# Expert weights in loads of 2 MiB with 16 KB per partition in seven of eleven slots

## The chip, the cores and the metric

The kernel runs on one core of one Trainium2 chip, in one launch. The metric is device time in microseconds of a run. The profile is of one execution; its span is the time from its first to its last instruction.

## The reference

One residual block on x of 256 tokens by 2048 features, all in float32, and a final RMS norm. Shown is the mixture of experts at its end, which the change is about.

```
h = rmsnorm(x); proj = h @ w_in               # 2048 x 11296: gates, SSD inputs, S5 input
... SSD branch -> w_a_up; S5 branch -> w_glu, w_b_up; both gated and summed
x = x + merged @ w_out
h2 = rmsnorm(x, norm_ffn_w)
grp   = argmax(h2 @ w_route_group + b)        # one of 4 groups of 8 experts
top 2 of the 8 experts of that group, softmax weights times the group's probability
for each of 32 experts e, for the tokens that chose it:
    y = (silu(h2 @ w_exp_gate[e]) * (h2 @ w_exp_up[e])) @ w_exp_down[e]
x = x + weighted sum of y;  out = rmsnorm(x, norm_final_w)
```

w_exp_gate and w_exp_up are 2048 x 512 for each expert, w_exp_down is 512 x 2048: 4 MiB each, 12 MiB an expert, 384 MiB for all 32. The other weights come to some 132 MiB.

## The kernel before

Tokens are 256, features 2048 = 16 k-tiles of 128 (KT). The first part streams the dense weights in units of 1 MiB (four k-tiles by 512 columns, rows of 2 KB). SyncE's queue (SP) loads a unit into one of three `raw` buffers; ScalarE and VectorE split it into a high and a low part in two halves, each into one of four `ws` buffers (`hi_next`, `lo_next`); TensorE multiplies (`mm_half`). The main loop (L1344) goes over half units; `hh` is the half, `i` the unit. At the first half of each unit it calls `st.load()` and then `ex_load(1)`. The last 16 units are `w_out`; its left operand lies in four `mg` tiles, and the last four units read one of them each.

The expert stage takes the experts four at a time, in 8 passes `p` (NQ), because at most 32 tokens an expert (CAP) are handled there and 4 x 32 = 128. A pass has: for each quarter `q` of the features, gate then up (L1601: four k-tiles by four experts, 32 matmul instructions as the profile counts them); silu and product; a transposition (L1630); four quarters of down (L1640; in the last pass L1658, in another order). Beside these run the selection of the next pass's tokens, `sel_gen`, in steps that `step(sel)` calls after each gate quarter and after two of the down quarters (four feature tiles a step: sixteen matmuls, L1532, that multiply columns of x1 by a one-hot matrix, then VectorE's scaling by the norm weight, L1536), and `comb` (L1555, L1557), which adds a pass's result to the sum, one quarter at a time after the next pass's gate and up groups. `warm` matmuls (L1437, L1672) are filler.

Which feature stands in which partition of a k-tile is free as long as the weights' rows agree: an expert load puts four successive feature rows of the weight into a partition (`(p k) n -> p k n`, p = 128), and the selection takes the columns of x1 in the same order, at a step of four.

Expert weights lie in `chunks` of 1 MiB: a quarter of one matrix. `EXF` is a queue of free slots; `ex_load(most)` takes slots from its front, each with the next chunk, and issues one DMA on SP; `EXT` remembers which slot holds which chunk; `ex_free` puts a read slot back at the end of the queue. Slots come into being in three ways: 11 tiles of their own, opened at the first unit of w_out in the place of tiles that are no longer needed (`open_out`, L1117); one `mg` tile after each of the last four units (`mg_slot`); `raw` and `ws` buffers when the dense stream lets go of them (`stream_slots`). The three `raw` slots are used once (`keep` false; they hold the sums `accx` and `y` later), the other 19 go round. The order of SP's issues is the order in the program; an issue waits until its slot's readers are done. The last pass's down chunks are cut otherwise, 256 rows by 1024 columns, in rows of 4 KB (L1303).

```
for p in passes:
    for q in 0..3:                     # gate, then up
        for w in (gate, up):
            32 matmuls over 4 k-tiles x 4 experts
            ex_free x 4;  ex_load()
            if w is gate: step(sel)
            one comb of the pass before
    silu, product, transposition
    for k in 0..3: 32 matmuls of down; ex_free x 4; ex_load(); step(sel) at k = 0, 2
```

Of the kernel before, what the change touches and what calls it, by code (L numbers as in the profile page):

```python
# [85 lines left out]
def hybrid_block(tc, A, cst_d, out_d, dbg=None, upto="all"):  # L86
# [949 lines left out]
    def need_v():  # L1036
# [28 lines left out]
    def ev_glu(j):  # L1065
        def f(acc):
# [43 lines left out]
    def open_out():  # L1110
        run_all("ev")
        close(late["gb_m"])
        close(late["ga_m"])
        close(s5_m)
        late["x1p_m"], p = pool("x1p", side="right")
        late["x1p"] = p
        for i in range(EX1):  # L1117
            ex1 = pool(f"ex1{i}", side="right")[1]
            EXF.append(slot_full(ex1, f"ew{i}"))

    def o_add(j, b, acc):
        x = late["x1"][:, b, 512 * j:512 * j + 512]
# [149 lines left out]
    def run_all(*names):  # L1272
        while any([advance(n) is not None for n in names]):
            pass


    chunks = [(w, EQ * p + e, q) for p in range(NQ) for ws in (("w_exp_gate", "w_exp_up"), ("w_exp_down",))
              for q in range(4) for w in ws for e in range(EQ)]
    tail_blocks = len(chunks) - 4 * EQ
    EXF = deque()  # L1280
    EXT = {}
    EXN = {"n": 0}

    def slot_full(pl, tag, keep=True, bufs=1):
        return lambda: pl.tile([P, 4, 512], F32, name="ew", tag=tag, bufs=bufs), keep

    def ex_load(most=99):
        while most > 0 and EXF and EXN["n"] < len(chunks):
            w, e, q = chunks[EXN["n"]]
            slot = EXF.popleft()  # L1290
            t = slot[0]()
            EXT[w, e, q] = (t, slot)
            src = A[w][0, e]
            if w != "w_exp_down":
                SP.dma_start(out=t, in_=src[q * 512:(q + 1) * 512].rearrange("(p k) n -> p k n", p=P))
            elif EXN["n"] < tail_blocks:
                SP.dma_start(out=t, in_=src[q * P:(q + 1) * P].rearrange("p (k n) -> p k n", n=512))
            else:
                h, m = divmod(q, 2)
                src = src[2 * P * m:2 * P * m + 2 * P, 1024 * h:1024 * h + 1024].rearrange("(k p) n -> p k n", p=P)  # L1300
                n = 512 if EXN["n"] == len(chunks) - 1 else 1024
                for c in range(0, 1024, n):
                    SP.dma_start(out=t.rearrange("p (k j) n -> p k (j n)", j=2)[:, :, c:c + n], in_=src[:, :, c:c + n])  # L1303
            EXN["n"] += 1
            most -= 1

    def ex_get(w, e, q):
        return lambda k: EXT[w, e, q][0][:, k]

    def ex_free(w, e, q):  # L1310
        slot = EXT.pop((w, e, q))[1]
        if slot[1]:
            EXF.append(slot)

    def mg_slot(i):
        j = i - (len(st.units) - 4)
        if j >= 0:
            EXF.append(slot_full(late["mgp"], f"mg{j}"))

    freed = {"raw": 0, "ws": 0}  # L1320

    def stream_slots():
        n = len(st.units)
        for tag, bufs, used, done in (("raw", RAWB, len(st.raw), st.nl == n),
                                      ("ws", WSB, len(st.wh) + len(st.split), st.nh == 2 * n)):
            while done and freed[tag] < bufs - used:
                EXF.append(slot_full(wp, tag, keep=tag == "ws", bufs=bufs))
                freed[tag] += 1

    S5_FROM = 9  # L1330
    nu = len(st.units)
# [12 lines left out]
    for hh in range(2 * last_unit):  # L1344
# [16 lines left out]
        if i == nu - 1:  # L1361
            if h == 1:
                last_unit_of_out()
                mg_slot(i)
            stream_slots()
            continue
        acc = mm_half(hh)
        stream_slots()
        if h == 1:
            mg_slot(i)  # L1370
        if i == S5_FROM and h == 0:
            queue("tab", tab_gen())
            queue("rot", rot_gen())
# [133 lines left out]


    nfw = cols[:, VEC["nffn"]:VEC["nffn"] + 16]
    GX = {}  # L1510

    def xg(k, w=1):
# [9 lines left out]
    def sel_gen(p):  # L1522
# [3 lines left out]
        for q in range(4):  # L1526
            n = 2 if p == 0 and q == 0 else 4
            for k0 in range(0, 4, n):
                pt = pe.tile([P, n, P], F32, name="pxg", tag="misc")
                for k in range(n):  # L1530
                    for b in range(2):
                        PE.matmul(pt[:, k], x1[:, b, 512 * q + k0 + k:512 * q + 512:4],  # L1532
                                  gx[:, b].rearrange("p e s -> p (e s)"),
                                  start=(k == 0 and b == 0), stop=(b == 1), skip_group_check=True)
                kk = 4 * q + k0
                V.tensor_tensor(xg(kk, n), pt, nfw[:, kk:kk + n, None].to_broadcast([P, n, P]), op=ALU.mult)  # L1536
# [39 lines left out]
    def step(g):  # L1576
        if g is not None:
            next(g, None)

    def take():  # L1580
        return EXF.popleft()[0]()

    sel = sel_gen(0)
    step(sel)
# [6 lines left out]
    for p in range(NQ):  # L1591
        last = p == NQ - 1
        pg_ = pe.tile([P, 512], F32, name="pg")
        pu_ = pe.tile([P, 512], F32, name="pu")
        for q in range(4):
            for w, o in (("w_exp_gate", pg_), ("w_exp_up", pu_)):
                ch = [ex_get(w, EQ * p + e, q) for e in range(EQ)]
                for k in range(4):
                    kk = 4 * q + k
                    for e, es in enumerate(cols_of):  # L1600
                        PE.matmul(o[es], xg(kk)[:, 0, es], ch[e](k), start=(kk == 0), stop=(kk == KT - 1))  # L1601
                for e in range(EQ):
                    ex_free(w, EQ * p + e, q)
                ex_load()
                if w == "w_exp_gate":
                    step(sel)
                if late_comb:
                    comb(*late_comb.pop(0))
        if last:
            wf = take()  # L1610
            for m in range(4):
# [15 lines left out]
            S.activation(rr[:, 0:1], kcol[:, 0:1], AF.Sqrt)  # L1627
        pt = pe.tile([P, 4, P], F32, name="pat", tag="misc")
        for k in range(4):
            PE.transpose(pt[:, k], sg[:, k * P:k * P + P], ident)  # L1630
# [148 lines left out]
```

## Time and profile before

| | |
|---|---|
| three runs | 1793.95, 1795.37, 1795.83 us; median 1795.37 |
| profiled execution | 1792.91 us, of which its span 1790.8 |
| TensorE busy (matmuls) | 1564.6 us, 87% of the span |
| VectorE, ScalarE, GpSimd busy | 783.7, 569.2, 130.9 us |
| DMA packets | 151,709, 566.05 MB, mean 316 GB/s |
| expert loads | 128 gate, 128 up, 127 down of 1024 KB and 2 of 512 KB; median 19.8 us from issue to landing |

A matmul's busy time is from its start to its modelled end, and these overlap; so 32 matmuls of 0.6 us each can pass in 3.6 us, and a high busy share is not a full engine. "PEld" is TensorE loading its stationary operand. The slices of the page are 44.8 us each. A wait in the profile names the engine that sat idle, the instruction that it then ran, and what released it. "SPq" lines are DMA issues on SyncE's queue: their time is the issue, not the transfer.

### The profile page before, as it was taken

The page shows a single profiled execution, that of the slowest core. Times are in us where ns is not written, and L with a number is a line of the kernel's source. Part 1 is how long each engine was busy: PE and PEld are TensorE (multiplying, and loading weights), DVE is VectorE, ACT ScalarE, POOL GpSimd, SP SyncE. Part 2 cuts the span into 40 slices and gives each one's busy share as a digit, 9 for nine tenths or more (in the row PEclk, how much of TensorE's full clock was granted, in tenths as well). Part 3 has the DMA queues.
Part 4 walks back from the last instruction along what each step waited for, and adds up shares of the span by engine and source line. Part 5 has one row for each costly group of instructions (what it writes and reads, how often), then busy time and mean ns, then how long its engine had stood idle before and what let it go on. Part 6 is the DMA issues. An engine that isn't in the chain of part 4 may idle for free. (4 is left out here: it accounts for less than half of the span.)

```text
span 1790.8 us, 25153 instructions
## 1 busy us (share of the span) xinstructions
PE 1564.6 (87%) x10511; PEld 1072.7 (60%) x10511; DVE 783.7 (44%) x1295; ACT 569.2 (32%) x811; POOL 130.9 (7%) x110
## 2 busy tenths in 40 slices
PE   9999999999999999999978688687687777877876
PEld 8999999999999998988523133132232331322332
DVE  5879888899899895754101101011011010110102
ACT  5465665768865865443000000000000000000003
POOL 3600000101112121000000000000000000000001
PEclk9999999999999998999989989999998998988988
DMA  9666555655566655698899999999999999999995
GB/s 256 215 210 214 187 188 177 196 176 184 182 206 199 190 189 189 213 390 316 340 422 421 421 422 420 421 421 421 421 421 422 421 421 421 422 421 421 421 415 230
DMA packets 151709, 566.05 MB, mean 316 GB/s; under 512 B 22316, under 2 KB 29012, under 8 KB 104232
## 3 DMA queue, kind: packets, MB, share of 16 engines
q1 hardware_dynamic: 149528, 558.74, 81.1%
q0 software_dynamic: 1632, 4.58, 0.9%
q8 instruction: 84, 1.38, 0.3%
q10 hardware_dynamic: 432, 1.08, 0.2%
q14 instruction: 33, 0.27, 0.0%
HBM read 558.04 MB, written 6.32 MB: 315 GB/s over the span
## 5 line engine op out<-in xcount | busy, mean ns | idle before, releaser
L237 PE MATMUL acc<-hTh,ws 128*128 128x256 f32 x1400 | 398.0, 284 | 0.0
L241 PE MATMUL acc<-hTh,ws 128*128 128x256 f32 x1400 | 394.7, 282 | 0.0
L239 PE MATMUL acc<-hTl,ws 128*128 128x256 f32 x1400 | 394.6, 282 | 0.0
L186 DVE TENSOR_TENSOR ws<-raw,ws 128x1024 fp32r<-128x1024 f32 x263 | 328.0, 1251 | 130.3 <-ACT ws L177 129.8
L177 ACT ACTIVATE ws<-raw 128x1024 fp32r<-128x1024 f32 x264 | 277.6, 1056 | 239.4 <-PE acc L241 185.0
L237 PEld LDWEIGHTS acc<-hTh,ws 128*128 128x128 f32 x1400 | 264.0, 189 | 3.9 <-issue 3.5
L239 PEld LDWEIGHTS acc<-hTl,ws 128*128 128x128 f32 x1400 | 263.9, 188 | 0.0
L241 PEld LDWEIGHTS acc<-hTh,ws 128*128 128x128 f32 x1400 | 263.8, 188 | 0.0
L1601 PE MATMUL pg<-ew,xg 128*32 128x512 f32 x1024 | 202.8, 675 | 68.0 <-DMA ew<-in_w_exp_gate_dram 67.8
L1536 DVE TENSOR_TENSOR xg<-pxg,cols 128x512 f32<-128x512 f32 (+1 forms) x33 | 22.3, 675 | 510.6 <-PE pxg L1532 510.6
L1640 PE MATMUL pd<-ew,cstB 128*32 128x512 f32 x896 | 162.8, 670 | 66.8 <-DMA ew<-in_w_exp_down_dram 62.0
L1601 PE MATMUL pu<-ew,xg 128*32 128x512 f32 x1024 | 153.0, 641 | 28.2 <-DMA ew<-in_w_exp_up_dram 28.2
L1601 PEld LDWEIGHTS pg<-ew,xg 128*32 128x32 f32 x1024 | 41.7, 121 | 217.5 <-DMA ew<-in_w_exp_gate_dram 129.0
L1546 ACT ACTIVATE cstC<-pgw 128x256 f32<-128x256 f32 x8 | 3.1, 384 | 522.9 <-PE pgw L1544 522.9
L1640 PEld LDWEIGHTS pd<-ew,cstB 128*32 128x32 f32 x896 | 35.0, 120 | 182.2 <-DMA ew<-in_w_exp_down_dram 116.4
L1532 PEld LDWEIGHTS pxg<-gx,x 128*128 128x128 f32 x512 | 122.0, 328 | 28.4 <-PE pg L1601 17.6
L1532 PE MATMUL pxg<-gx,x 128*128 128x128 f32 x512 | 128.6, 404 | 1.9 <-DVE gx L1519 1.3
L1601 PEld LDWEIGHTS pu<-ew,xg 128*32 128x32 f32 x1024 | 35.0, 115 | 127.6 <-issue 75.8
L727 POOL TENSOR_TENSOR s5p<-s5p 128x512 f32<-128x512 f32 x32 | 66.0, 2062 | 398.9 <-DVE s5p L726 398.9
L1642 ACT ACTIVATE y<-pd 128x512 f32<-128x512 f32 x28 | 16.7, 597 | 240.3 <-PE pd L1640 240.3
L1619 DVE TENSOR_TENSOR cstB<-cstB,pu 128x512 f32<-128x512 f32 x8 | 5.5, 686 | 197.4 <-PE pu L1601 152.5
L1555 PE MATMUL pcb<-y,cstC 128*128 128x512 f32 x128 | 69.0, 628 | 22.9 <-DVE accx L1557 21.9
(364 smaller groups left out, 1948.0 us busy)
## 6 DMA issues: line engine op xcount, KB each, us to landing
ew<-in_w_exp_gate_dram SPq DMA_DIRECT2D x128, 1024.0 KB, 19.8
ew<-in_w_exp_up_dram SPq DMA_DIRECT2D x128, 1024.0 KB, 19.8
ew<-in_w_exp_down_dram SPq DMA_DIRECT2D x127, 1024.0 KB, 19.8
raw<-in_w_in_dram SPq DMA_DIRECT2D x87, 1024.0 KB, 4.9
raw<-in_w_a_up_dram SPq DMA_DIRECT2D x16, 1024.0 KB, 5.1
raw<-in_w_out_dram SPq DMA_DIRECT2D x16, 1024.0 KB, 7.3
raw<-in_w_b_up_dram SPq DMA_DIRECT2D x8, 1024.0 KB, 5.1
bc<-acs_d POOLq DMA_DIRECT2D x8, 512.0 KB, 4.3
```

Of the source, the lines that this page charges most:

```text
L177: S.activation(ws[:, 0], self.raw[i][:, 2 * h:2 * h + 2], AF.Copy)
L186: (eng or V).tensor_tensor(ws[:, 1], self.raw[i][:, 2 * h:2 * h + 2], ws[:, 0].bitcast(F32), op=ALU.subtract)
L237: PE.matmul(acc[:, cb], wh[:, k2, cs], hi, start=fk and cb % 2 == 0, stop=False, skip_group_check=True)
L239: PE.matmul(acc[:, cb], wh[:, k2, cs], lo, start=False, stop=False, skip_group_check=True)
L241: PE.matmul(acc[:, cb], wl[:, k2, cs], hi, start=False, stop=lk, skip_group_check=True)
L727: G.tensor_tensor(pp[:, 0:2], pp[:, 0:2], pp[:, 2:4], op=ALU.add)
L1532: PE.matmul(pt[:, k], x1[:, b, 512 * q + k0 + k:512 * q + 512:4], gx[:, b].rearrange("p e s -> p (e s)"), start=(k == 0 and b == 0), stop= ...
L1536: V.tensor_tensor(xg(kk, n), pt, nfw[:, kk:kk + n, None].to_broadcast([P, n, P]), op=ALU.mult)
L1555: PE.matmul(pc, GX[p][:, b], ACC["y"][:, n], start=True, stop=True)
L1601: PE.matmul(o[es], xg(kk)[:, 0, es], ch[e](k), start=(kk == 0), stop=(kk == KT - 1))
L1640: PE.matmul(pd[n][es], aT[:, k, es], ch[e](n), start=(k == 0), stop=(k == 3))
L1642: S.activation(ACC["y"][:, n], pd[n], AF.Copy)
```

## The change

The unit of loading becomes half a matrix, 2 MiB: 1024 feature rows of gate or up, with eight successive rows (16 KB) in a partition, or 256 rows of down, two successive ones (16 KB) in a partition. `loads` lists them, each with the keys of its two chunks of 1 MiB. A slot is now a `Slot` of two parts. Where it is `flat` (16 KB in one piece of a partition) one DMA fills it; else two DMAs of 1 MiB (8 KB a partition) do. There are eleven slots: five pairs from the first tile, which is now one tile of 11 MiB (its eleventh part is `late["odd"]`), two from the `mg` tiles, which are now two pairs (these seven are flat), and four in parts: odd with a raw buffer, two raw buffers (both used once), and twice two ws buffers. Nine go round. A slot is free when both its parts have been read.

In a pass the two quarters of a half follow one another: gate q0, gate q1, up q0, up q1, and so on. In the first pass, after gate q0 and after gate q1, the part of the slot just read is refilled at once, by 1 MiB, with the loads 11 to 14. `ex_load(1)` adds a credit of half a load, so the main loop loads 2 MiB at every second unit. The last pass's down weights stay in 1 MiB pieces of 4 KB rows, with successive rows in a partition. The selection takes x1's columns at a step of eight, the transposition (L1630) those of the product at a step of two, and the norm weight is loaded once more in that order (`nfw8`, one DMA on GpSimd's queue). `take()` hands out parts of 1 MiB, first the odd one.

```diff
-    cols = const.tile([P, P], F32, name="cols")
+    cols = const.tile([P, P + 16], F32, name="cols")
...
+        G.dma_start(out=cols[:, P:].rearrange("p (q k) -> p q k", k=8),
+                    in_=A["norm_ffn_w"][0].rearrange("(q p k) -> p q k", p=P, k=8))
         nf = VEC["nffn"]
...
-        late["mg"] = [p.tile([P, 2, 4, T], F32R, name="mg", tag=f"mg{i}") for i in range(4)]
+        mg = [p.tile([P, 2, 2, 4, T], F32R, name="mg", tag=f"mg{i}") for i in range(2)]
+        late["mg"] = [mg[i // 2][:, i % 2] for i in range(4)]
...
-        for i in range(EX1):
-            ex1 = pool(f"ex1{i}", side="right")[1]
-            EXF.append(slot_full(ex1, f"ew{i}"))
+        ex1 = pool("ex1", side="right")[1].tile([P, EX1, 4, 512], F32, name="ew")
+        for i in range(0, EX1 - 1, 2):
+            EXF.append(Slot(ex1[:, i:i + 2].rearrange("p a k n -> p (a k n)")))
+        late["odd"] = ex1[:, EX1 - 1]
...
+    def rows_of(w, e, q):
+        src = A[w][0, e]
+        if w == "w_exp_down":
+            return src[2 * P * q:2 * P * q + 2 * P].rearrange("(p k) n -> p (k n)", k=2)
+        return src[1024 * q:1024 * q + 1024].rearrange("(p k) n -> p (k n)", k=8)
...
+    def part_load(slot, i, load):
+        keys, joint = load
+        t = slot.parts[i]
+        EXT[keys[i]] = t, slot
+        slot.left += 1
+        if joint is not None:
+            SP.dma_start(out=t.rearrange("p k n -> p (k n)"), in_=joint[:, 2048 * i:2048 * i + 2048])
+            return
...
+    def ex_load(most=None):
+        EXN["credit"] = 999 if most is None else min(EXN["credit"] + most, 2)
+        while EXN["credit"] > 0 and EXF and EXN["n"] < len(loads):
+            slot, load = EXF.popleft(), loads[EXN["n"]]
+            if slot.flat is not None and load[1] is not None:
+                slot.left = 2
+                for i in range(2):
+                    EXT[load[0][i]] = slot.parts[i], slot
+                SP.dma_start(out=slot.flat, in_=load[1])
             else:
...
+                for i in range(2):
+                    part_load(slot, i, load)
             EXN["n"] += 1
-            most -= 1
+            EXN["credit"] -= 2
...
+        if freed["raw"] == 0 and st.ns >= 2 * n - 4:
+            EXF.append(Slot(parts=[late["odd"], one("raw", RAWB)], keep=False))
+        if freed["mg"] == 0 and done >= 2 * n - 4:
+            EXF.append(Slot(two("mg0")))
+        if freed["raw"] == 1 and st.ns == 2 * n:
+            EXF.append(Slot(parts=[one("raw", RAWB), one("raw", RAWB)], keep=False))
+        if freed["ws"] == 0 and done >= 2 * n - 2:
+            EXF.append(Slot(parts=[one("ws", WSB), one("ws", WSB)]))
+        if freed["ws"] == 2 and done == 2 * n:
+            EXF.append(Slot(parts=[one("ws", WSB), one("ws", WSB)]))
+            EXF.append(Slot(two("mg1")))
...
-                    PE.matmul(pt[:, k], x1[:, b, 512 * q + k0 + k:512 * q + 512:4],
+                        c0 = 1024 * (q // 2) + 4 * (q % 2) + k0 + k
+                    PE.matmul(pt[:, k], x1[:, b, c0:c0 + 1017:8],
...
-        for q in range(4):
+        for q2 in range(2):
             for w, o in (("w_exp_gate", pg_), ("w_exp_up", pu_)):
+                for q in (2 * q2, 2 * q2 + 1):
...
+                    if p == 0 and q < 2 and w == "w_exp_gate":
+                        for e in range(EQ):
+                            sl = EXT.pop((w, e, q))[1]
+                            sl.left -= 1
+                            part_load(sl, q, loads[EXN["n"] + e])
+                        if q == 1:
+                            EXN["n"] += EQ
+                    else:
+                        for e in range(EQ):
+                            ex_free(w, EQ * p + e, q)
+                        ex_load()
```

## Rows read from the trace of the kernel before

**Rows 1.** The page's second part: GB/s in each of 40 equal slices

```profile
GB/s 256 215 210 214 187 188 177 196 176 184 182 206 199 190 189 189 213 390 316 340 422 421 421 422 420 421 421 421 421 421 422 421 421 421 422 421 421 421 415 230
```

**Rows 2.** Windows; columns: stretch, length, busy PE, PEld, DVE, ACT, POOL, PEclk, DMA share, GB/s

```profile
764.00:796.00 32.00, 32.00 (x149) 25.92 (x149) 15.89 (x17) 12.77 (x14) 0.00 (x0) 1.00 1.03 399
...
850.00:860.00 10.00, 8.09 (x48) 4.94 (x48) 2.78 (x11) 0.20 (x1) 0.56 (x1) 0.83 0.37 150
...
860.00:870.00 10.00, 10.00 (x77) 5.54 (x73) 3.07 (x18) 0.20 (x1) 0.00 (x0) 1.00 0.81 330
...
880.00:1720.00 840.00, 652.03 (x3380) 233.91 (x3376) 88.17 (x212) 28.39 (x50) 0.00 (x0) 0.93 1.01 421
...
1730.00:1760.00 30.00, 23.84 (x132) 9.85 (x128) 0.69 (x1) 6.15 (x10) 0.00 (x0) 0.70 1.03 409
```

**Rows 3.** Waits of all engines; columns: total us, times, longest

```profile
PEld pg L1601 <- DMA ew<-in_w_exp_gate_dram: 129.0, 65, 2.4
```

**Rows 4.** Timeline of TensorE at the expert stage's start: start us, us, instruction

```profile
856.44 4.09 PE L1601 MATMUL pg<-ew,xg 128*32 128x512 f32 x32
...
860.46 4.00 PE L1532 MATMUL pxg<-gx,x 128*128 128x128 f32 x16
...
864.39 3.64 PE L1601 MATMUL pu<-ew,xg 128*32 128x512 f32 x32
```

**Rows 5.** Timeline of SyncE's issues between the stages

```profile
843.47 0.91 SPq L1295 DMA_DIRECT2D ew<-in_w_exp_up_dram  x2
...
860.55 0.80 SPq L1295 DMA_DIRECT2D ew<-in_w_exp_up_dram  x2
```

**Rows 6.** Timeline of TensorE at the end

```profile
1759.59 3.62 PE L1658 MATMUL pd<-ew,cstB 128*32 128x512 f32 x26 [1.51 <-DMA ew<-in_w_exp_down_dram]
...
1770.34 3.64 PE L1658 MATMUL pd<-ew,cstB 128*32 128x512 f32 x32
```

**Rows 7.** DMA packets from 880 to 1720 us

```profile
DMA packets 48545, 353.78 MB, mean 421 GB/s; under 512 B 5387, under 2 KB 5387, under 8 KB 5387
```

**Rows 8.** Timeline of VectorE, first selection step of the loop

```profile
864.50 0.69 DVE L1536 TENSOR_TENSOR xg<-pxg,cols 128x512 f32<-128x512 f32 x1 [7.53 <-PE pxg L1532]
```

**Rows 9.** Timeline of TensorE: groups at the low clock, and a round's steps

```profile
1008.58 6.50 PE L1601 MATMUL pu<-ew,xg 128*32 128x512 f32 x26 [1.44 <-DMA ew<-in_w_exp_up_dram]
...
1058.26 5.56 PE L1601 MATMUL pg<-ew,xg 128*32 128x512 f32 x26 [0.58 <-DMA ew<-in_w_exp_gate_dram]
...
1067.59 1.02 PE L1555 MATMUL pcb<-y,cstC 128*128 128x512 f32 x2
...
1069.40 1.12 PE L1555 MATMUL pcb<-y,cstC 128*128 128x512 f32 x2 [0.78 <-DVE accx L1557]
```

**Rows 10.** The page's sixth part: issues, KB each, median us to landing

```profile
raw<-in_w_in_dram SPq DMA_DIRECT2D x87, 1024.0 KB, 4.9
```

**Rows 11.** SyncE's own waits

```profile
SPq L1295 <- DMA ew<-in_w_exp_gate_dram: 176.1, 84, 2.2
```

**Rows 12.** Timeline of SyncE's issues at the start of w_out

```profile
748.39 0.34 SPq L1295 DMA_DIRECT2D ew<-in_w_exp_gate_dram  x1
...
754.92 0.37 SPq L168 DMA_DIRECT2D raw<-in_w_out_dram  x1
```

**Rows 13.** Timeline of VectorE there

```profile
752.53 1.22 DVE L1096 TENSOR_TENSOR mg<-gb,mg 128x1024 fp32r<-128x1024 f32 x1 [1.13 <-ACT mg L1094]
```

**Rows 14.** Timeline of GpSimd

```profile
691.24 1.15 POOL L351 TENSOR_TENSOR cstB<-cstB,cols 128x576 f32<-128x576 f32 x1 [6.20 <-DVE ws L186]
```

**Rows 15.** Weight loads by line: count, duration ns min/median/max, first and last start

```profile
L1532 PEld LDWEIGHTS pxg<-gx,x x512: 307/329/332, 851.3 to 1705.9; 128*128 128x128 f32 x171
...
L1437 PEld LDWEIGHTS warm<-x,cstA x32: 192/192/192, 845.6 to 849.0; 128*128 128x128 f32 x32
```

**Rows 16.** Windows of TensorE alone: stretch, length, busy, PEclk, DMA share, GB/s

```profile
936.00:938.00 2.00, 1.52 (x2) 0.50 1.03 430
...
944.00:946.00 2.00, 2.00 (x9) 1.00 1.00 418
```

More of the change, by code (lines that the diff above doesn't have):

```diff
@@ L1274, in run_all, with last_down @@
             pass
-    chunks = [(w, EQ * p + e, q) for p in range(NQ) for ws in (("w_exp_gate", "w_exp_up"), ("w_exp_down",))
-              for q in range(4) for w in ws for e in range(EQ)]
-    tail_blocks = len(chunks) - 4 * EQ
+    def rows_of(w, e, q):
[3 more added lines that the diff above has]
+        return src[1024 * q:1024 * q + 1024].rearrange("(p k) n -> p (k n)", k=8)
+    def last_down(e, q):
+        h, m = divmod(q, 2)
+        return A["w_exp_down"][0, e][2 * P * m:2 * P * m + 2 * P, 1024 * h:1024 * h + 1024].rearrange(
+            "(p k) n -> p k n", k=2)
@@ new lines, in hybrid_block @@
+    loads = []
+    for p in range(NQ):
+        for q in range(2):
+            for w in ("w_exp_gate", "w_exp_up"):
+                loads += [([(w, EQ * p + e, 2 * q), (w, EQ * p + e, 2 * q + 1)], rows_of(w, EQ * p + e, q))
+                          for e in range(EQ)]
+        w = "w_exp_down"
+        if p < NQ - 1:
+            loads += [([(w, EQ * p + e, 2 * q), (w, EQ * p + e, 2 * q + 1)], rows_of(w, EQ * p + e, q))
+                      for q in range(2) for e in range(EQ)]
+        else:
+            loads += [([(w, EQ * p + e, q), (w, EQ * p + e + 1, q)], None) for q in range(4) for e in range(0, EQ, 2)]
@@ L1280, in hybrid_block @@
     EXF = deque()
     EXT = {}
[L1282 to L1297, printed above, removed]
-            else:
[L1299 to L1303, printed above, removed]
+    EXN = {"n": 0, "credit": 0}
@@ new lines, in hybrid_block, with __init__ @@
+    class Slot:
+        def __init__(self, flat=None, parts=None, keep=True):
+            self.flat = flat
+            self.parts = parts or [flat[:, 2048 * i:2048 * i + 2048].rearrange("p (k n) -> p k n", n=512)
+                                   for i in range(2)]
+            self.keep = keep
+            self.left = 0
+    def part_load(slot, i, load):
[6 more added lines that the diff above has]
+            return
+        src = last_down(*keys[i][1:])
+        n = 512 if keys[i] == ("w_exp_down", NE - 1, 3) else 1024
+        for c in range(0, 1024, n):
+            SP.dma_start(out=t.rearrange("p (k j) n -> p k (j n)", j=2)[:, :, c:c + n], in_=src[:, :, c:c + n])
@@ L1311, in ex_free, with one, two, stream_slots @@
         slot = EXT.pop((w, e, q))[1]
-        if slot[1]:
+        slot.left -= 1
+        if slot.keep and slot.left == 0:
             EXF.append(slot)
[L1315 to L1322, printed above, removed]
-        n = len(st.units)
[L1324 to L1328, printed above, removed]
+    def one(tag, bufs):
+        return wp.tile([P, 4, 512], F32, name="ew", tag=tag, bufs=bufs)
+    def two(tag):
+        return late["mgp"].tile([P, 4096], F32, name="ew", tag=tag)
+    freed = {"raw": 0, "ws": 0, "mg": 0}
+    def stream_slots(done):
+        n = len(st.units)
+        if st.nl < n:
+            return
+        if freed["raw"] == 0 and st.ns >= 2 * n - 4:
+            EXF.append(Slot(parts=[late["odd"], one("raw", RAWB)], keep=False))
+            freed["raw"] = 1
+        if freed["mg"] == 0 and done >= 2 * n - 4:
+            EXF.append(Slot(two("mg0")))
+            freed["mg"] = 1
+        if freed["raw"] == 1 and st.ns == 2 * n:
+            EXF.append(Slot(parts=[one("raw", RAWB), one("raw", RAWB)], keep=False))
+            freed["raw"] = 3
+        if freed["ws"] == 0 and done >= 2 * n - 2:
+            EXF.append(Slot(parts=[one("ws", WSB), one("ws", WSB)]))
+            freed["ws"] = 2
+        if freed["ws"] == 2 and done == 2 * n:
+            EXF.append(Slot(parts=[one("ws", WSB), one("ws", WSB)]))
+            EXF.append(Slot(two("mg1")))
+            freed["ws"] = 4
     S5_FROM = 9
@@ L1509, in hybrid_block @@
     nfw = cols[:, VEC["nffn"]:VEC["nffn"] + 16]
+    nfw8 = cols[:, P:P + 16]
     GX = {}
@@ L1578, in step @@
             next(g, None)
+    spare = [late["odd"]]
     def take():
-        return EXF.popleft()[0]()
+        if not spare:
+            spare.extend(EXF.popleft().parts)
+        return spare.pop()
     sel = sel_gen(0)
```

34 lines of the change are left out of this document (15 added, 19 removed).

## The prediction

> **What bounds the kernel now.** I read the page's 40 slices first. The transfer rate wanders around 200 GB/s for the first 16 slices and stands at 421 or 422 GB/s from slice 21 to slice 38 [rows 1]. So there are two kernels in one: a first half that waits for engines, and an expert stage in which the DMA engines are full. The windows confirm it: from 880 to 1720 us the DMA share is 1.01 at 421 GB/s [rows 2]. Second, the waits say what ends last there: TensorE's weight loads wait 129.0 us for gate weights to land [rows 3]. One group of 32 matmuls takes 3.64 us when fed [rows 4], and its four 1 MiB loads take 4 x 2.49 = 10.0 us at 421 GB/s. The stage is bound by bytes per second; the time changes if the rate changes, or if the DMA queue runs dry.
>
> Two places where it is not full matter. Between the stages all 22 slots are full and nothing may be loaded: the slice 850 to 860 moves 150 GB/s, 860 to 870 moves 330 GB/s [rows 2]. Read as full-rate stretches, that is data until 853.6 us and again from 862.2 us, after the first refills were issued at 860.55 [rows 5], so 1.7 us from issue to data. At the end, the third down group waits for a landing (1759.59), and the last one, at 1770.34, for no DMA but for TensorE's own work in between [rows 6]. The chain starts with a landing, so an earlier landing moves all of it.
>
> **The rate.** From 880 to 1720 us there were 48,545 packets, 5,387 of them under 512 B and none between that and 8 KB [rows 7]. The others are 43,158, eight for each small one: a load of 1 MiB is, on each of 16 engines, eight packets of 8 KB, one per partition row, and one small one at its end. So a row is a packet, and a flat load of the change makes it 16 KB. What a packet costs beyond its bytes is read from stretches with other row lengths. Per 8 KB and engine: at 421 GB/s 311.3 ns (16 x 8192 / 421). From 1730 to 1760 us, where the last down loads have rows of 4 KB, 409 GB/s or 320.5 ns [rows 2]. One packet more costs 9.2 ns; the bytes cost 302.1. A third stretch tests the line: from 764 to 796 us half the bytes are w_out in 2 KB rows (four packets), half expert rows of 8 KB; the line gives (302.1 + 4 x 9.2 + 311.3)/2 = 325.1 ns, 403 GB/s; the row has 399 [rows 2]. So 16 KB rows should run at 302.1 + 4.6 = 306.7 ns, 427.4 GB/s: per MiB 2.453 us instead of 2.491, 0.0373 us less.
>
> How many loads are flat? In the order in which slots come free, loads 0 to 4, 6 and 10 of the first eleven go into flat slots; they land before the full stretch and save nothing. Loads 11 to 14 are the halves. From load 15 the nine kept slots take turns: flat, flat, two of halves, five flat. Loads 15 to 183 are 18 rounds of 9 and seven more: 18 x 7 + 5 = 131 flat loads, 262 MiB. The last eight stay in pieces as before. 262 x 0.0373 = 9.8 us.
>
> The small packet is now one per 2 MiB. No row prices it alone: from 0 (it hides) to the 9.2 ns of a packet. I take 9.2, since every packet that the windows price costs that; 131 x 9.2 ns = 1.2 us. Removed in total: 11.0 us, bounds 9.8 and 11.0 if rows stay packets.
>
> **The start of the stage.** Before, group after group gave four slots back. Now gate q0 and q1 run one behind the other, then up q0 and q1, and a slot of 2 MiB comes back when both halves are read. By the durations of before [rows 4, 8]: gate q0 ends at 860.46; first halves of loads 11 to 14 flow from 862.2 to 872.15. The selection step (sixteen matmuls) ends at 864.39. Gate q1 needs its result, which VectorE has at 865.19 (0.69 us); before, up q0 stood in this hole, so TensorE loses 0.85 us. Gate q1 (3.64) ends at 868.9 and the second halves keep the queue full until 882.1. Step, up q0, up q1: 868.9 + 3.9 + 3.64 + 3.64 = 880.1. The up weights were in slots 4 to 7, of which 5 and 7 are lent and don't return, so two slots come back: data at 881.8, in time, lasting 9.8 us to 891.9. Gate q2, step, VectorE, gate q3 (3.64 + 3.9 + 0.85 + 3.64) end at 892.1, the next data come at 893.8. Gap: 1.9 us, the price of this edit. From there four slots come back at a time and the queue gets ahead.
>
> **The steady rounds.** Nine slots: when the fourth load of a group has landed, five are in flight, 10 MiB, 24.5 us. Refill comes after both halves: 5.56 (26 matmuls, at the low clock), 4.00, then 1.02 + 0.78 + 1.12 for the sums, 3.64 for the second half [rows 4, 9]: 16.2 us. From issue to landing a queue that is not full needs 4.9 us for 1 MiB [rows 10], of which 2.5 are bytes, so some 2.3 us of lag. 24.5 - 16.2 - 2.3 leaves 6.0 us; the queue doesn't run dry. Before, a refill waits for a DMA eight issues back (176.1 us in 84 waits for gate loads alone [rows 11]); those waits go, and waits for TensorE stand in their place, hidden by the same 6 us.
>
> **What I cost at nothing.** The first fill: the last slots (two halves of ws, two more, the second mg pair) are free at 843.5, when the kernel before issued its last loads [rows 5]. With what is still in flight some 6 MiB remain then, 14.9 us, until 858.5, and the refills' data come at 862.2. If the fill ends later, each us late is a us lost, up to 3. The one large ex1 tile: its first load went out at 748.39, and may now wait for VectorE's last read of gb, 752.53 + 1.22 [rows 12, 13]. Behind it on SyncE stands a w_out load that itself went out at 754.92, so no issue is later. The 2 MiB ahead of it may make it land 2.5 us later; four ws buffers hold three halves ready for TensorE, which hides it, and without that cover it would be the 2.5 us. The small norm load is one more issue on POOL; behind it stands only the scaling of the router weights, at 691.24 [rows 14]; its first reader belongs to w_out, whose first unit comes with the issue at 748.39, so a few us there move nothing. Fewer and larger issues on SyncE save only time that is covered.
>
> [...] The selection reads x1 at a step of 8 floats instead of 4. One such weight load takes 329 ns at step 4; a contiguous one in the filler takes 192 [rows 15]. Step 8 stands in no row: between 329 and, doubling, 658. I take 329, the nearest row. [...]
>
> **Sum.** -9.8 - 1.2 + 1.9 = -9.1 us. The profiled execution took 1792.91 us, 2.1 of them outside its span of 1790.8, and would take 1783.8. The median of three runs, 1795.37, is 2.5 above it; against it the forecast is 1786.3.
>
> **Rivals.**
> Half. The 4 KB stretch reads rows a whole matrix row apart and is the tail; some of its loss may be that and not packets. For it: the 2 KB mix came out 4 GB/s under the line, so the line isn't exact. Against: it errs to the other side. With half the saving, -5.5 + 1.9 = -3.6: 1791.8. [...]
>
> Rows are cut. If a 16 KB row goes as two packets of 8 KB, the rate stays; the gap less the small packets leaves +0.7: 1796.1. For it: no packet over 8 KB is in the trace. Against: 2, 4 and 8 KB rows all went whole.
>
> Slower: the strided selection. If step 8 doubles the weight load, a step of sixteen takes 5.3 us more. In the start chain each refill hangs on a step: gaps of 3.8, 6.5 and 7.5 us, 17.8 in all, -11.0 + 17.8 = +6.8: 1802.2. It decides from about 515 ns a load on (3 us a step, gaps of 11). For it: steps 1 to 4 cost 137 ns, and a straight line through them gives 512 (gaps 10.6). Against: no row says that the cost goes on growing past step 4, and the reads keep their number.
>
> [...]
>
> **Chances.** Forecast 0.57, own range 1783 to 1790; half 0.13; rows cut 0.13; strided 0.10; low clock 0.07. Two in ten outside: 1782 to 1799. This kernel's measurement tells about 0.2%, 3.6 us, from no change. Faster: 0.57 + 0.07 of half = 0.64. Same: 0.06 of half, the cut rows and 0.03 of strided = 0.22. Slower: 0.07 + 0.07 = 0.14.
>
> **What would show it.** Right: 16 KB packets in the expert stage, 427 to 428 GB/s over flat loads and some 426 over all until the tail, a first dip near 892 of about 2 us, the same PE chain from the third down group on. Wrong: rate of 421 (cut), selection weight loads over 500 ns with dips near 872, 886 and 902, or slices of the steady stage under 420 with SyncE waiting for TensorE while nothing is in flight.

## The result: 11 us less

The changed kernel takes 1783.88 us (median of 6 runs, 1782.58 to 1788.01) against 1794.84 for the kernel before (6 runs beside them): ratio 0.9946 [0.9936, 0.9955]. The profiled execution took 1782.58 us, its span 1780.8; that is 10.0 less than the 1790.8 before.

The slices of the page, after. From slice 22 to slice 38 the steady stage stands at 425 to 427 where [rows 1] had 420 to 422, and slice 21 at 424.

```profile
GB/s 257 215 210 213 192 188 179 185 181 191 184 207 184 203 177 194 201 405 273 364 424 427 425 426 425 426 426 425 426 426 426 427 425 427 426 426 426 425 416 229
```

The windows, after, with the columns of [rows 2]. The first two 10 us stretches of the stage move 209 and 365 GB/s (150 and 330 before), the long one 426. PEclk, the granted TensorE clock as a share of full speed, is 0.86 there where it was 0.93, and the DMA share is 1.01 all the same. In 764 to 796 TensorE now has 0.92 us of idle time; it had none.

```profile
764.00:796.00 32.00, 31.08 (x144) 24.86 (x143) 16.74 (x19) 12.19 (x14) 0.00 (x0) 1.00 1.03 408
850.00:860.00 10.00, 9.41 (x50) 5.18 (x49) 1.20 (x4) 0.00 (x0) 0.00 (x0) 0.66 0.50 209
860.00:870.00 10.00, 9.22 (x57) 6.39 (x56) 3.07 (x18) 0.20 (x1) 0.00 (x0) 1.00 0.93 365
...
880.00:1720.00 840.00, 622.80 (x3374) 233.57 (x3370) 88.21 (x212) 28.80 (x51) 0.00 (x0) 0.86 1.01 426
```

The DMA packets from 880 to 1720 us, after [rows 7]: 30,467 in place of 48,545 for slightly more bytes. So the rows of 16 KB did go out whole.

```profile
DMA packets 30467, 357.59 MB, mean 426 GB/s; under 512 B 3355, under 2 KB 3355, under 8 KB 3868
```

The waits, after [rows 3, 11]. TensorE still waits for landings, in fewer and longer pieces (21 waits for gate weights in place of 65). SyncE, which waited for earlier loads to land, now waits in the main for TensorE to give slots back. That is the replacement the prediction named, and with the DMA share at 1.01 it costs nothing.

```profile
PEld pd L1707 <- DMA ew<-in_w_exp_down_dram: 136.2, 34, 7.2
...
PEld pg L1658 <- DMA ew<-in_w_exp_gate_dram: 67.1, 21, 4.8
...
SPq L1338 <- PE pd L1707: 149.9, 13, 16.5
SPq L1338 <- PE pu L1658: 137.4, 13, 14.5
```

TensorE at the stage's start, after [rows 4]. Gate q0 and q1 follow one another with the step between; the 0.78 us hole in front of gate q1 is there as forecast (0.85).

```profile
854.98 4.65 PE L1658 MATMUL pg<-ew,xg 128*32 128x512 f32 x32
859.56 4.07 PE L1584 MATMUL pxg<-gx,x 128*128 128x128 f32 x16
864.41 3.64 PE L1658 MATMUL pg<-ew,xg 128*32 128x512 f32 x32 [0.78 <-DVE xg L1588]
...
871.98 7.07 PE L1658 MATMUL pu<-ew,xg 128*32 128x512 f32 x64
878.87 3.62 PE L1658 MATMUL pg<-ew,xg 128*32 128x512 f32 x32
```

TensorE at the end, after [rows 6]. The last up group began at the low clock (granted 0.50 from 1718 to 1722 us; 58 matmuls in 9.45 us), and 96 matmuls of down go by with no wait for a landing. So in this execution the last landing that TensorE waited for is one of up weights, and from there on its own work ends the stage.

```profile
1719.20 9.45 PE L1658 MATMUL pu<-ew,xg 128*32 128x512 f32 x58 [3.89 <-DMA ew<-in_w_exp_up_dram]
1741.31 12.19 PE L1725 MATMUL pd<-ew,cstB 128*32 128x512 f32 x96 [0.69 <-ACT cstB L1699]
...
1760.64 3.64 PE L1725 MATMUL pd<-ew,cstB 128*32 128x512 f32 x32
```

Selection weight loads, after [rows 15]: the median at step 8 is 334 ns, against 329 at step 4.

```profile
L1584 PEld LDWEIGHTS pxg<-gx,x x512: 312/334/338, 849.6 to 1705.7; 128*128 128x128 f32 x171
```

**Where the 10.0 us of the span went.** Four marks in both traces split it: the first w_out matmul (748.2 before, 745.3 after), the filler (845.61, 843.98), the first gate group (856.44, 854.98), and the start of the last down group (1770.34, 1760.64). By the differences of the stretches: ahead of w_out -2.9, w_out +1.3, the routing between +0.2, the expert stage -8.2, behind it -0.3. The stage scatters between executions of the kernel before: 913.9 us here, 916.4 in e5, 916.3 in e12.

### The profile page after: what moved, and what is told of

Read it like the earlier page. It is cut to its first block, busy times and chain, and to the rows that moved or that the text cites. A ratio compares the mean times of both kernels' runs of the same rounds, so it can differ in the third digit from the quotient of the medians.

```text
span 1780.8 us, 24833 instructions
## 1 busy us (share of the span) xinstructions
PE 1530.1 (86%) x10511; PEld 1071.9 (60%) x10511; DVE 783.2 (44%) x1295; ACT 569.2 (32%) x811; POOL 132.8 (7%) x111
## 3 DMA queue, kind: packets, MB, share of 16 engines
q10 hardware_dynamic: 432, 1.08, 0.2%
## 5 line engine op out<-in xcount | busy, mean ns | idle before, releaser
L1707 PE MATMUL pd<-ew,cstB 128*32 128x512 f32 x896 | 167.3, 757 | 103.0 <-DMA ew<-in_w_exp_down_dram 98.2
L1658 PE MATMUL pg<-ew,xg 128*32 128x512 f32 x1024 | 160.8, 689 | 54.8 <-DMA ew<-in_w_exp_gate_dram 47.8
L1658 PE MATMUL pu<-ew,xg 128*32 128x512 f32 x1024 | 141.6, 651 | 32.2 <-DMA ew<-in_w_exp_up_dram 32.2
L1658 PEld LDWEIGHTS pg<-ew,xg 128*32 128x32 f32 x1024 | 37.0, 122 | 167.0 <-issue 91.2
L1609 DVE TENSOR_TENSOR accx<-accx,pcb 128x512 f32<-128x512 f32 x56 | 38.5, 687 | 105.3 <-PE pcb L1607 105.3
```

Of the source, the lines that this page charges most:

```text
L1609: V.tensor_tensor(a, x1[:, b, 512 * n:512 * n + 512] if p == 0 else a, pc, op=ALU.add)
L1707: PE.matmul(pd[n][es], aT[:, k, es], ch[e](n), start=(k == 0), stop=(k == 3))
```

## Experiments

Times stand beside runs of the kernel before on the same chip, which had medians of 1794.6 (e1 to e4), 1794.39 (e5 to e8) and 1794.86 (e9 to e12).

**e1, the changed kernel again.**

> The changed kernel as it is, beside the runs below. Packets theory (the gain is the cost of packets): 1784, some 10 to 11 us under the kernel before, expert stage at 426 GB/s. If the part of the gain that lies ahead of the expert stage (the first w_out matmul came 2.8 us earlier in the one profile) is chance, this profile's first w_out matmul may lie anywhere from 745 to 748 us and the gain of the stage from its first gate group on stays at 8 us.

1785.08 us, ratio 0.9943 [0.9930, 0.9957]. The result stands. First w_out matmul at 745.1, first gate group to last down group 906.0 us (905.7 in the first profile, 913.9 before).

**e2, the whole change, but every slot filled by two loads of 1 MiB in rows of 8 KB.**

```diff
-            if slot.flat is not None and load[1] is not None:
+            if False:
```

> Same slots, same order, same halves at the start, but every flat slot is filled by two loads of 1 MiB with rows of 8 KB. Packets theory: the rate falls back to 421 GB/s and 262 MiB cost 11.0 us more than in the changed kernel: 1795. Rival (the ring and the new order bring the gain, by fewer waits of SyncE on DMA): 1784 with 421 GB/s or less.

1795.41 us, ratio 1.0005 [0.9996, 1.0014]. Without the long rows nothing of the gain is left. The new order, the halves and the larger slots together cost 0.8 us, between a gain of 0.7 and a cost of 2.5 by the interval.

**e3, loads of 2 MiB, but as two rows of 8 KB in each partition.**

```diff
-        return src[1024 * q:1024 * q + 1024].rearrange("(p k) n -> p (k n)", k=8)
+        return src[1024 * q:1024 * q + 1024].rearrange("(a p k) n -> p a (k n)", a=2, k=4)
...
-                SP.dma_start(out=slot.flat, in_=load[1])
+                SP.dma_start(out=slot.flat.rearrange("p (a m) -> p a m", a=2), in_=load[1])
```

(down likewise; the selection goes back to a step of four)

> Loads of 2 MiB in the same slots, but a partition takes two rows of 8 KB from places 512 feature rows apart (128 for down), and the selection goes back to a step of four floats. Packets theory: the row length is what counts, so 302.1 + 9.2 - 0.6 = 310.7 ns for 8 KB, 422 GB/s, 9.6 us over the changed kernel: 1793.5. Rival (the size of a load counts): 426 GB/s and 1784. Rival on the selection: if the step of eight costs anything, this kernel's selection loads take less than 333 ns and the start dips go.

1794.38 us, ratio 0.9995 [0.9986, 1.0004]. The load's size is not what pays; the row's is. Step 4 in place of 8 shows no gain either: a selection weight load takes 330 ns (334 at step 8), and the start is no smoother (360 and 369 GB/s at 872 to 876 and 884 to 888 us).

**e4, rows of 4 KB everywhere, those of the halves too.**

```diff
-        return src[1024 * q:1024 * q + 1024].rearrange("(p k) n -> p (k n)", k=8)
+        return src[1024 * q:1024 * q + 1024].rearrange("(i a p k) n -> p i a (k n)", i=2, a=2, k=2)
```

> Loads of 2 MiB in the same slots, rows of 4 KB (four to a partition); the rows stand in another order than the selection's columns, so the products are of other pairs than the reference's. Packets theory, line with 9.2 ns a packet: 302.1 + 18.4 - 0.6 = 319.9 ns, 410 GB/s in flat loads, 28.9 us over the changed kernel: 1813. If the 409 GB/s of the last down loads was due to their place and not their rows: well under that, 1784 to 1795.

1819.10 us, ratio 1.0135 [1.0119, 1.0150]. My figure left out that the loads in halves had also gone to 4 KB; with them the line gives 1818.4. The packets of the changed kernel, e2, e3 and e4, each from 1000 to 1700 us:

```profile
DMA packets 25040, 298.09 MB, mean 426 GB/s; under 512 B 2778, under 2 KB 2778, under 8 KB 2778
```

```profile
DMA packets 40399, 294.36 MB, mean 421 GB/s; under 512 B 4490, under 2 KB 4490, under 8 KB 4490
```

```profile
DMA packets 38649, 294.51 MB, mean 421 GB/s; under 512 B 2721, under 2 KB 2721, under 8 KB 2721
```

```profile
DMA packets 72506, 286.36 MB, mean 409 GB/s; under 512 B 2664, under 2 KB 2664, under 8 KB 72481
```

Bytes by 700 us and 16 engines give, per 8 KB: 320.4 ns in rows of 4 KB, 311.7 (e2) and 311.5 (e3) in rows of 8 KB. After, 307.8 over all; two loads in nine go into halves at 311.6, so the 16 KB rows ran at (9 x 307.8 - 2 x 311.6)/7 = 306.7; e8, where every load in this stretch has them, gives 306.9. Per packet that is 8.8 ns from 4 to 8 KB and 9.4 to 9.8 from 8 to 16 KB: nearly the straight line of the prediction. Gate and up rows of 4 KB, which follow one another in e4, take the time that the last down loads took before (320.5), whose rows lie a whole matrix row apart. So it was the length of those rows and not their place. e3 has 1769 small packets fewer than e2, 111 per engine; at 9.2 ns they would be 1.0 us of the 700. The two differ by 0.15 MB, 0.4 us.

**e5, the kernel before once more.**

> The kernel before, once more, for a second profile. If the 2 to 3 us that the changed kernel was ahead at its first w_out matmul (745.3 and 745.1 us against 748.2) are chance, this profile's may lie near 746; if they belong to the change, near 748. From the first gate group to the third down group's last landing it takes 903 us as before.

1796.17 us, span 1794.1. First w_out matmul at 748.8. To the third down group's last landing it takes 903.9 us from the first gate group's start, as expected; but the 26 matmuls behind that landing took 5.32 us in place of 3.62, and to the last down group it is 916.4 us, 2.5 more than in the first profile before.

**e6, without refilling by halves at the start.**

```diff
-                    if p == 0 and q < 2 and w == "w_exp_gate":
+                    if False:
```

> The changed kernel without the refill by halves: the first four slots come back after both quarters. Theory of the start: the first refill's data come 8.3 us later, the gap near 892 of 2 us goes, four more flat loads save 0.3 us: 6 us over the changed kernel, 1790. Rival (the queue has enough in hand, the halves do nothing): 1784.

1791.89 us, ratio 0.9988 [0.9979, 0.9997], so 6.8 us more than e1 and 8.1 more than e7. The windows of e6: the engines all but stand still from 860 to 870 (21 GB/s), where the changed kernel moved 365 GB/s.

```profile
850.00:860.00 10.00, 8.71 (x48) 5.03 (x48) 2.23 (x9) 0.00 (x0) 0.24 (x1) 0.83 0.59 249
860.00:870.00 10.00, 9.22 (x58) 6.20 (x54) 3.07 (x18) 0.20 (x1) 0.00 (x0) 1.00 0.11 21
870.00:880.00 10.00, 10.00 (x84) 4.79 (x87) 0.69 (x1) 0.00 (x0) 0.00 (x0) 1.00 0.93 392
```

Without the halves some 7 us of the saving go into this one hole.

**e7, 1 MiB at every unit of w_out and not 2 MiB at every second.**

```diff
+        if EXN["open"] is not None and (most is None or most):
+            part_load(EXN["open"], 1, loads[EXN["n"]])
...
+                EXN["open"] = EXF.popleft()
+                part_load(EXN["open"], 0, loads[EXN["n"]])
```

> The changed kernel, but during w_out the slots are filled by 1 MiB at every unit instead of 2 MiB at every second one. In the changed kernel ScalarE waited 12.4 us in 4 waits for w_out weights there, and the stretch from the first w_out matmul to the filler took 98.7 us against 97.4 before. Theory (a load of 2 MiB ahead of a w_out load makes it late): those waits go and the stretch takes 97.4: 1783, 1.3 us less. Rival (it is the late first load behind the one large tile): the waits stay.

1783.75 us, ratio 0.9937 [0.9923, 0.9951]. w_out to the filler takes 97.4 us, as before, against 98.7 after. ScalarE's waits from 745 to 845 us, of the changed kernel and of e7:

```profile
ACT ws L177 <- DMA raw<-in_w_out_dram: 12.4, 4, 5.6
```

```profile
ACT ws L177 <- DMA raw<-in_w_out_dram: 3.7, 2, 1.9
```

So the +1.3 us in w_out is the 2 MiB load in front of a w_out load. e11, with the same edit, takes 97.3; the other changed kernels 98.5 to 99.1. The total gains less than a measurement tells: from the first gate group to the last down group e7 takes 907.3 us, 1.6 more. Its second gate group ran at a lower clock (granted 0.70 from 864 to 868 us, 1.00 in the changed kernel): its first 28 matmuls took 4.81 us where all 32 took 3.64 in the first profile after, and from 872 to 876 us the rate was 354 GB/s where it was 426 there. In e2, e6, e9 and e10 the group took 3.64 us; in e3 the granted clock was 0.77 from 864 to 868 us and 0.80 from 868 to 872; and in e11, with e7's edit:

```profile
863.36 5.26 PE L1669 MATMUL pg<-ew,xg 128*32 128x512 f32 x32 [0.78 <-DVE xg L1599]
```

Whether e7's edit brings this on is not shown.

**e8, the two pairs of ws buffers made flat too, so all nine kept slots take 16 KB rows.**

```diff
-            EXF.append(Slot(parts=[one("ws", WSB), one("ws", WSB)]))
+            t = wp.tile([P, 2, 4096], F32, name="ew", tag="ws", bufs=1)
+            for j in range(2):
+                EXF.append(Slot(t[:, j]))
```

(the four ws buffers are one tile from the start of the kernel on, and both its slots stand behind the second mg pair)

> The changed kernel with the four ws buffers as one tile that becomes two flat slots after the last unit, so that all nine slots that go round are flat. Packets theory: 38 more flat loads, 76 MiB x 0.0373 us = 2.8 us less, at 427.4 GB/s from 1000 to 1700 us; the first fill now ends some 860 us, which may cost 1 us: 1781 to 1782. Rival (a steady 426 GB/s is the ceiling): 1784 at 426 GB/s.

1785.21 us, ratio 0.9946 [0.9932, 0.9960]: no gain. The rate rose as expected (299.00 MB from 1000 to 1700, 427 GB/s). But one ws tile is free only at the very end of w_out, and the first fill stalls there. By 920 us e8 had moved 205.79 MB and the changed kernel 208.65; its first gate group started 4.2 us later (859.19), which is 1.8 MB, and the other 1.1 MB are 2.5 us that the stall and a second dip at 896 us cost. From 920 to 1700 us e8 gains 1.08 MB (333.21 against 332.13), worth 2.5 us, as much as the stall and the dip had cost. At the end TensorE waits 1.50 us for the third down group's landing (0.57 in e1, nothing in the first profile after). So the gain of the rate is more than gone: the stage takes 907.7 us, 905.7 in the first profile after. (The profile is of e8's slowest run, 1788.46 us.) The later start does not come from w_out, which takes 98.5 us to the filler (98.7 after): the first w_out matmul is at 749.4. Two windows of e8:

```profile
844.00:848.00 4.00, 3.79 (x28) 3.33 (x26) 1.84 (x7) 1.62 (x4) 0.00 (x0) 1.00 0.47 111
...
896.00:900.00 4.00, 4.00 (x42) 1.30 (x42) 0.00 (x0) 2.26 (x3) 0.00 (x0) 1.00 0.78 246
```

**e9, a ring of eight slots** (one pair of ws buffers is used once).

```diff
-            EXF.append(Slot(parts=[one("ws", WSB), one("ws", WSB)]))
+            EXF.append(Slot(parts=[one("ws", WSB), one("ws", WSB)], keep=False))
             EXF.append(Slot(two("mg1")))
```

> The second pair of ws buffers is used once and not refilled: a ring of eight slots, seven of them flat, in place of nine with seven flat. Theory (6 us of slack in a ring of nine, worked out from row lengths and TensorE's durations): when the fourth load of a group lands, four are in flight, 19.6 us; the refill comes 16.2 us after the landing at worst and lands data 2.3 us later, so 1.1 us are left, the queue stays full, and 17 more loads have 16 KB rows, which is 17 x 2 x 0.0373 = 1.3 us less: 1782.5 to 1784. Rival (the slack was already nearly used in a ring of nine, since TensorE runs at its lower clock in much of the stage): the queue runs dry for some 2 to 5 us at each of the seven passes' down sums, 14 to 35 us: 1797 to 1818, with slices under 420 GB/s once a pass.

1788.82 us, ratio 0.9968 [0.9958, 0.9978]. Between the two theories. At the down sums of a pass the refill goes out at 1442.23, 16.55 us after the landing at 1425.68 (16.2 was the sum). The engines then run thin, but don't stop. Windows of e9 there, and over the steady stretch:

```profile
1440.00:1444.00 4.00, 4.00 (x32) 2.26 (x24) 0.00 (x0) 0.00 (x0) 0.00 (x0) 1.00 0.98 373
1444.00:1448.00 4.00, 3.22 (x13) 2.39 (x13) 1.38 (x2) 0.00 (x0) 0.00 (x0) 1.00 0.94 393
...
1000.00:1700.00 700.00, 522.72 (x2778) 191.16 (x2770) 72.52 (x172) 23.14 (x42) 0.00 (x0) 0.85 1.00 423
```

These two windows lose 0.8 us against 426 GB/s. So where 1.1 us should have been left, 0.8 is missing, and the ring of nine, one load of 4.9 us longer, has about 4.1 us to spare there, not 6.0. The 4.1 is an estimate from one such round. Seven rounds of 0.8 us less 1.3 for the longer rows are 4.3 us; the medians of the change and of e1 are 4.9 and 3.7 under e9's.

**e10, a ring of seven** (both pairs used once; the last pass asks for loads after each down quarter).

> Both pairs of ws buffers are used once: a ring of seven flat slots, every later load in 16 KB rows; the last pass also asks for loads after each quarter of its down groups, since its pieces would not all have slots before. Theory (the same sum as for the ring of eight): three loads in flight last 14.7 us, against 16.2 + 2.3 us to the refill's data in the round with the down sums: dry for 3.8 us in seven passes, 27 us, and in rounds of 13 us up to 0.6 us more each, so with 2.8 us less for the row length 1808 to 1830. Rival (refills don't set the rate, the row length alone does): 1781 to 1782.

1852.90 us, ratio 1.0324 [1.0308, 1.0340]: the mechanism, and well over the size. Windows of e10, one pass:

```profile
1392.00:1400.00 8.00, 5.51 (x36) 1.25 (x28) 0.42 (x3) 0.87 (x2) 0.00 (x0) 0.84 0.52 184
1456.00:1460.00 4.00, 3.73 (x26) 0.71 (x18) 0.00 (x0) 1.79 (x3) 0.00 (x0) 1.00 0.50 131
1476.00:1484.00 8.00, 7.22 (x45) 3.61 (x45) 1.46 (x3) 0.00 (x0) 0.00 (x0) 1.00 0.57 199
```

Against 427 GB/s they lose 4.6, 2.8 and 4.3 us. The third is the round I had summed (3.8 foreseen). The other two I had put at 0.6: they are gate q3 and the last down quarter, with a selection step inside and matmuls at the low clock (32 in 5.34 us and 26 in 6.10). The queue runs dry three times in this pass, not once. It is one of the worse passes: the 396 GB/s of e10 from 1000 to 1700 us are 51 us lost in some six passes, 8.5 a pass where this one loses 11.7.

**e11, e7's edit, and the final norm's broadcast moved behind the second up group of the last pass.**

```diff
+                    if last and q == 1 and w == "w_exp_up":
+                        wf = take()
...
```

> The changed kernel with two edits: in the w_out stage the weight slots are filled by 1 MiB at each unit and not by 2 MiB at every second, and in the last pass the four-piece broadcast of the final norm stands behind the second up group and no longer between the last up group and the sums. Theory: the first is worth what it was alone (1783.75 against 1785.08), the second at most 0.5 us, as the tail is bound by TensorE and the broadcast's sixteen small products take half a microsecond of it: 1783.0 to 1783.8. Rival (the last down group's landing sets the end, as in the kernel before): the second is worth nothing, 1783.7.

1786.96 us, ratio 0.9960 [0.9946, 0.9973]. It is no better than e7 or the change, and perhaps 2 us worse. TensorE of e11 at the end, and then of e1:

```profile
1731.35 5.65 PE L1736 MATMUL pd<-ew,cstB 128*32 128x512 f32 x36 [0.69 <-ACT cstB L1710]
...
1751.29 5.02 PE L1736 MATMUL pd<-ew,cstB 128*32 128x512 f32 x26 [1.52 <-DMA ew<-in_w_exp_down_dram]
...
1763.44 3.64 PE L1736 MATMUL pd<-ew,cstB 128*32 128x512 f32 x32
```

```profile
1739.16 10.10 PE L1725 MATMUL pd<-ew,cstB 128*32 128x512 f32 x70 [0.69 <-ACT cstB L1699]
1749.83 3.62 PE L1725 MATMUL pd<-ew,cstB 128*32 128x512 f32 x26 [0.57 <-DMA ew<-in_w_exp_down_dram]
1760.58 3.64 PE L1725 MATMUL pd<-ew,cstB 128*32 128x512 f32 x32
```

The down groups start 8 us earlier than in e1 and then wait 1.5 us for each landing. The rival holds: the landings set the end, with TensorE close behind them. Of the 2.9 us by which e11's last group is later, 1.5 are the third group's landing: 1.0 of them because e11 had moved 208.24 MB by 920 us and e1 208.69 (at 426 GB/s). The other 1.4 are the 26 matmuls behind that landing: 5.02 us, 3.62 in e1; the granted clock was 0.83 from 1750 to 1760 us, 1.00 in e1. That the moved broadcast brought the low clock on is not shown. In e12 TensorE had waited 1.5 us for each of the last two landings as well, and took 3.62:

```profile
1763.02 3.62 PE L1660 MATMUL pd<-ew,cstB 128*32 128x512 f32 x26 [1.52 <-DMA ew<-in_w_exp_down_dram]
```

**e12, the kernel before with the wider constants' tile and the second norm load.**

> The kernel before, with the two edits of the change that lie ahead of the w_out stage and no others: the constants' tile is 64 bytes a partition wider, which moves every tile behind it, and the norm weights are loaded into it a second time on GpSimd's queue. Theory (the 1 to 3.5 us by which the changed kernels reach their first w_out matmul earlier come from these): 1792 to 1793.5, first w_out matmul near 746. Rival (they are scatter between executions, or come with the loads that follow): 1795, first w_out matmul at 748.

1794.57 us, ratio 0.9997 [0.9988, 1.0006], first w_out matmul at 749.2. These two edits are not what shortens the part ahead of w_out.

## Why the prediction was right

The forecast was 1783.8 us for the profiled execution and 1786.3 against the median; measured were 1782.58 and 1783.88, near the lower end of the range (1783 to 1790). Sign and size are right, and the main term is shown; the smaller terms were off, and they and a part that was not forecast cancel in good part.

**Rate, -9.8: right.** From 920 to 1700 us neither kernel's queue runs dry. The packets of before, and of after, from 920 to 1700:

```profile
DMA packets 45082, 328.53 MB, mean 421 GB/s; under 512 B 5005, under 2 KB 5005, under 8 KB 5005
```

```profile
DMA packets 27961, 332.13 MB, mean 426 GB/s; under 512 B 3109, under 2 KB 3109, under 8 KB 3109
```

3.60 MB more at 426 GB/s are 8.5 us. Loads 15 to 183, 354 MB, make it 9.1; against e2, which moved 327.98 MB in that stretch, 10.5. So rate and small packets together are worth 9 to 10.5 us, where the sum had 9.8 and 1.2. e2, e3 and e4 show that it is the packet of a row: rival "half" falls (306.7 ns; half would be 309.0), and "rows are cut" falls by the packet count.

**Small packets, -1.2: not seen.** e3 against e2 prices them at 0.4 us where 1.0 was due, but kernels with 8 KB rows differ by as much among themselves (294.83 MB before, 294.31 in e12, both from 1000 to 1700). The 306.7 ns of the 16 KB rows is the line without any saving; with it 306.1 was due. So the bound of nothing was nearer than the 9.2 ns that I took.

**Start, +1.9: right in kind, too large.** Both kernels had the same bytes in at 860 us (183.75 before, 183.76 after). From there to 920 us, the packets of before and of after:

```profile
DMA packets 3336, 24.36 MB, mean 406 GB/s; under 512 B 365, under 2 KB 365, under 8 KB 365
```

```profile
DMA packets 2559, 24.89 MB, mean 415 GB/s; under 512 B 272, under 2 KB 272, under 8 KB 272
```

After has 0.53 MB more, but its first gate group started 1.46 us earlier (0.62 MB), and some 50 us at the higher rate are worth 0.25 MB: 0.34 MB short, 0.8 us. (e5, the kernel before again, is 0.36 MB short of the first profile by the same count, so this is 0.8 give or take as much.) The chain came as forecast: the up groups end 23.9 us after the first gate group's start (23.7 forecast). The gap near 892 us didn't: from 888 to 896 the rate is still some 409 GB/s, 0.3 us lost (e1: 340 from 892 to 896, 0.8 us). The step of the prediction that failed here is "a slot of 2 MiB comes back when both halves are read". SyncE's issues, after [rows 5]:

```profile
882.50 0.33 SPq L1323 DMA_DIRECT2D ew<-in_w_exp_down_dram  x1
...
890.93 1.28 SPq L1323 DMA_DIRECT2D ew<-in_w_exp_down_dram  x3
892.30 1.76 SPq L1338 DMA_DIRECT2D ew<-in_w_exp_down_dram  x2
```

The loads there go into pairs of ws buffers by two DMAs each, and the first of these DMAs waits only for gate q2's part. It goes out at 882.50, right behind gate q2, and its 1 MiB lasts 2.5 us: longer than the gap of 1.9.

0.8 - 9.1 = -8.3 agrees with the -8.2 of the stage, more closely than the scatter of the stage warrants: against e5 or e12 the stage is 10.7 us shorter, and not 8.2.

**The end: not the chain that was forecast.** By the prediction the third down group's landing moves the whole chain behind it. In the first profile after no down group waits for a landing, in e1 the third one waits 0.57 us (1.51 before). TensorE and the loads end level.

**Costed at nothing.** The w_out loads behind 2 MiB were not covered: +1.3 us, inside the bound of 2.5, and e7 takes it away. The selection at step 8 was: 334 ns, so the strided rival falls, and a straight line from 192 ns to 329 did not go on.

**Low clock: there, and harmless in the steady rounds of a ring of nine.** PEclk fell from 0.93 to 0.86, and groups of 26 matmuls took 5 to 6.5 us in many rounds, but not whole rounds, as the chance of 0.07 supposed: from 1065 to 1070 us, in a group that took 5.12, the granted clock was 0.66, and from 1070 to 1100 us it was 1.00. The refill stayed ahead by about 4 us, as estimated from e9, where the sum had 6.0. Where no slack has built up yet, at the stage's start, a gate group at the low clock does cost (5.26 us against 3.64 in e11).

**Not forecast: the part ahead of w_out, -2.9.** Three profiles with before's code there (e12's counted) have the first w_out matmul at 748.2 to 749.2 us; ten of the changed kernels at 745.1 to 747.5, and e8 at 749.4. e12 shows that two of the edits alone don't bring it. The mg tiles as two pairs and the larger ex1 tile were not tried alone. What the traces do show is the granted clock. Over the first 100 us, long before the first edited load, it lies anywhere from 0.97 to 1.00 among ten of these profiles (0.98 in the first of before and of after). From 600 to 700 us it is 0.95 in both profiles of before and in three of the changed kernels (e3, e7, e8: first w_out matmul at 746.9 to 749.4), and 0.97 in the other five of the ten (the first after, e1, e2, e4, e6: 745.1 to 747.1). In that stretch TensorE gets 11 matmuls further after than before, some 1.3 us at 0.12 us each. So about half of the 2.9 us goes with a clock that scatters between executions of the changed kernels too; whether the change has a share in it, and where the rest comes from, stays open. Before, and after:

```profile
600.00:700.00 100.00, 94.04 (x773) 91.70 (x772) 77.52 (x122) 67.07 (x100) 23.82 (x19) 0.95 0.59 190
```

```profile
600.00:700.00 100.00, 93.93 (x784) 91.63 (x783) 78.99 (x121) 67.06 (x98) 25.42 (x20) 0.97 0.58 190
```

**Sum.** -9.1 (rate) + 0.8 (start) + 1.3 (w_out) + 0.2 - 2.9 - 0.3 = -10.0, against a forecast of -9.1. Without the part ahead of w_out it would be -7.1, so the forecast came as near as it did with some luck.

## What to carry to other kernels

When the DMA engines are full, fit bytes and packets separately from two stretches with different row lengths of the same trace, and extrapolate: here a line through 4 and 8 KB gave 306.7 ns for 16 KB, and 306.7 to 306.9 came out. Read from rates that are rounded to 1 GB/s, such a line is good to about 1 ns, so the last digit is luck. Then count what the longer row costs in granularity: slots twice as large come back half as often, so price the first refill after any stop (here 7 to 8 us without halves) and the slack of the ring by its worst rounds, all of them, with matmuls at the low clock. A saving on an engine that ends level with the loads (e11) or a rate bought by freeing buffers later (e8) came to nothing.

## What the runs showed of the hardware that was not expected

A load's size, 1 or 2 MiB, made no difference to the rate at the same row length (e2, e3: 421 GB/s both). A lower mean clock of TensorE from 880 to 1720 us (0.86 against 0.93) went with a shorter time. It came with the new order of groups and not with the rate: e2, at 421 GB/s and with no gain, has 0.86 too (from 1000 to 1700 us).
